# One encoder layer on one core: the buffers of the split weight blocks, each 64 bytes longer

## The chip, the cores and the metric

The kernel runs on one core of one Trainium2 chip. The metric is the device time of one execution in microseconds (us), the median of the runs shown. Lower is better.

## The reference

One layer of a hybrid encoder on 1024 tokens of width 1024, all in float32. Two gated feed-forward layers (`_swiglu`) stand around a mixing layer with bidirectional retention and a two-dimensional neighbourhood attention; each part has an RMS norm before and after it.

```python
def _swiglu(x, w_in, w_out):
    g, u = jnp.split(x @ w_in, 2, axis=-1)
    return (jax.nn.silu(g) * u) @ w_out
...
    h = _swiglu(_rms_norm(x, ffn1_pre_norm[l]), ffn1_w_in[l], ffn1_w_out[l])
    x = x + 0.5 * _rms_norm(h, ffn1_post_norm[l])
    m = _token_mixing(_rms_norm(x, mix_pre_norm[l]), w_mix_in[l], ret_decay_fwd[l], ret_decay_bwd[l],
                      na_rel_bias[l], w_ret_out[l], w_na_out[l], w_mix_out[l], pos)
    x = x + _rms_norm(m, mix_post_norm[l])
    h = _swiglu(_rms_norm(x, ffn2_pre_norm[l]), ffn2_w_in[l], ffn2_w_out[l])
    x = x + 0.5 * _rms_norm(h, ffn2_post_norm[l])
```

The weights are w_in 1024 x 5632, w_out 2816 x 1024, w_mix_in 1024 x 6656 and three output projections.

## The kernel before, in words

Every large product is made in a split form. A float32 operand a is written as h + l: h is a rounded to the matmul's input type (float32r) and l is the rest. A product of two split operands is three matmuls, h h, h l and l h (`mm3`, lines 86 to 90), summed in one bank of PSUM. A matmul has a stationary operand, 128 x 128, which a weight load (LDWEIGHTS, engine PEld in the profile) brings into the array first, and a moving operand of up to 512 columns, which streams through it. The weight load of a matmul runs while the matmul before it streams. In the profile's rows the moving operand stands first: `ps<-a11h,wh` has a11h moving and wh stationary.

Weight blocks come from HBM into `wraw` (`raw`, lines 70 to 73) and are split by `piece` (lines 75 to 80): ScalarE (ACT) writes the rounded block to a buffer `wh` and VectorE (DVE) the rest to a buffer `wl`, both 128 partitions x 512 columns. There are eight buffers of each, used in turn, and a piece takes one of each, so the two always have the same number. In the first feed-forward products and in the projections that use `Pairs` (a Winograd form: seven block products in place of eight), slices of 128 columns of `wh` and `wl` are stationary, and the split activations a11, a12, a22, s1 to s4 move; there a piece serves 4 slices x 3 matmuls = 12. In the second feed-forward products (`ffn_out`) the pieces move and the gated activations g are stationary, in 4 slices, again 12 matmuls for a piece. In the mixing layer's projections the pieces move or stand still as the place wants it, with 6 to 24 matmuls for a piece.

The order of the instructions is the order of the code, apart from a few high-priority regions; `Filler` interleaves projections with attention and retention.

Where the operands lie matters to the change. The tiles are given out from both ends of each partition's memory. Their lengths are whole multiples of 512 bytes per partition, but for small ones and for two paddings (`edge`, 128 bytes, and `pad` in `mix`, 160 bytes). In the built program all of wraw, wh, wl, t2, the a and s operands, g, xy, gh, gl, pth, vh, k, q and nearly every other large tile begin at an address that leaves 352 when divided by 512; the identity matrix of the transposes leaves 128, and `ev` in the mixing pool 0. This remainder is called the residue below.

One place reads within a tile at another residue: in the neighbourhood attention's scores (`scores` in `na_cores`, line 909) the moving operand is a window of k, 12 rows of 32 columns (128 bytes out of every 256), which begins 0, 32, 96 or 128 bytes behind the tile's start, by the column block (`KEY_OFF`); the stationary q stands at 352 there too. Line 65 has the subtraction of the split with a scale, `ql<-qraw,qh`: qraw is read in pieces of 64 bytes, 256 bytes apart, and qh and ql without a gap, so the two sources' residues differ by another amount from piece to piece.

Of the kernel before, what the change touches and what calls it, by code (L numbers as in the profile page):

```python
# [11 lines left out]
F32R = mybir.dt.float32r  # L12
# [6 lines left out]
P = 128  # L19
# [19 lines left out]
class Core:  # L39
# [34 lines left out]

    def piece(self, src, eng=None):

        h = self.wpool.tile([P, 512], F32R, tag="wh", name="wh", bufs=8)
        l = self.wpool.tile([P, 512], F32R, tag="wl", name="wl", bufs=8)
        self.split(h, l, src, eng=eng)
        return h, l  # L80

# [1502 lines left out]
```

## Time and profile before

| | |
|---|---|
| median of three timed runs | 2288.16 us (2287.96 to 2288.34) |
| span of the profiled execution, first to last instruction | 2285.9 us |
| what lies around the span (median less span) | 2.3 us |
| TensorE (PE) busy | 2210.8 us, 97% of the span, 10232 matmuls |
| weight loads (PEld) busy | 1828.4 us, 80% |
| VectorE (DVE), ScalarE (ACT), GpSimd (POOL) busy | 74%, 44%, 28% |
| mean granted TensorE clock | 0.991 of full speed |

The profile gives no time of its own for the profiled execution beside its span. A matmul's row gives the time from its start to its modelled end; matmuls overlap, so the time that one adds to a dense stretch is the distance between two starts, which is a window's length by the number of matmuls in it.

### The profile page before, as it was taken

To read this page: it belongs to the slowest core of one execution; us is meant where nothing else is said; L and a number is where in the kernel's file an instruction comes from. 1 tells how busy PE (TensorE), PEld (TensorE's weight loads), DVE (VectorE), ACT (ScalarE), POOL (GpSimd) and SP (SyncE) were. 2 spreads that over 40 slices of the span, in tenths; PEclk is the share of its full clock that TensorE was granted. 3 is DMA by queue.
4 is the path that set the end of the run, shared out by engine and by line. 5 is a ranking of instruction groups with operands and counts; after the bars stand their busy time and mean duration, and the time that the engine had idled before them with its cause. 6 is when DMAs were issued, how large, how long until landed. Compare 5 with 4: busy or idle time off the path is not lost. (4 is left out here: it accounts for less than half of the span.)

```text
span 2285.9 us, 30140 instructions
## 1 busy us (share of the span) xinstructions
PE 2210.8 (97%) x10232; PEld 1828.4 (80%) x10232; DVE 1686.3 (74%) x2928; ACT 1000.7 (44%) x2086; POOL 650.9 (28%) x779
## 2 busy tenths in 40 slices
PE   6899999999998999999999999999899999999998
PEld 5688888888787887778888888887578888888886
DVE  7998878755568667969876678537988888886444
ACT  5444434332344322259875665315544343433232
POOL 1121212169424133401101222101531212125942
PEclk9999999999999999999999999999999999999999
DMA  6353434597555452357754566766434444349865
GB/s 248 134 193 134 175 129 175 213 379 282 203 178 172 149 184 79 111 187 255 219 165 165 166 212 233 288 219 206 171 133 171 166 150 163 140 144 369 303 224 181
DMA packets 150090, 444.11 MB, mean 194 GB/s; under 512 B 18800, under 2 KB 46576, under 8 KB 147824
## 3 DMA queue, kind: packets, MB, share of 16 engines
q1 hardware_dynamic: 111216, 314.23, 40.2%
q0 software_dynamic: 38720, 127.96, 14.6%
q8 instruction: 81, 1.33, 0.2%
q14 instruction: 73, 0.60, 0.1%
HBM read 305.80 MB, written 140.51 MB: 195 GB/s over the span
## 5 line engine op out<-in xcount | busy, mean ns | idle before, releaser
L62 DVE TENSOR_TENSOR wl<-wraw,wh 128x512 fp32r<-128x512 f32 x512 | 363.9, 730 | 83.1 <-ACT wh L61 82.3
L61 ACT CAST wh<-wraw 128x512 fp32r<-128x512 f32 x516 | 297.9, 618 | 213.5 <-DVE wraw L530 63.8
L88 PE MATMUL ps<-wh,g 128*128 128x512 f32 x484 | 188.7, 390 | 0.0
L89 PE MATMUL ps<-wl,g 128*128 128x512 f32 x484 | 188.5, 389 | 0.0
L90 PE MATMUL ps<-wh,g 128*128 128x512 f32 x484 | 188.3, 389 | 0.0
L552 ACT ACTIVATE c<-c 128x512 f32<-128x512 f32 x88 | 55.5, 632 | 205.8 <-DVE c L517 105.8
L62 DVE TENSOR_TENSOR wl<-w,wh 128x512 fp32r<-128x512 f32 x77 | 75.5, 993 | 84.9 <-ACT wh L61 83.9
L62 DVE TENSOR_TENSOR wl<-x,wh 128x512 fp32r<-128x512 f32 x77 | 80.5, 1066 | 75.8 <-ACT wh L61 74.8
L61 ACT CAST wh<-t 128x512 fp32r<-128x512 f32 x58 | 36.0, 621 | 191.1 <-DVE t L511 191.0
L88 PE MATMUL ps<-a11h,wh 128*128 128x512 f32 x276 | 111.7, 405 | 7.5 <-ACT wh L61 7.3
L90 PE MATMUL ps<-a11h,wl 128*128 128x512 f32 x276 | 109.7, 398 | 5.0 <-DVE wl L62 4.9
L88 PE MATMUL ps<-a22h,wh 128*128 128x512 f32 x280 | 109.9, 392 | 0.0
L90 PE MATMUL ps<-a22h,wl 128*128 128x512 f32 x280 | 109.2, 390 | 0.6 <-DVE wl L62 0.6
L89 PE MATMUL ps<-a11l,wh 128*128 128x512 f32 x276 | 109.5, 397 | 0.1
L88 PE MATMUL ps<-a12h,wh 128*128 128x512 f32 x276 | 108.9, 394 | 0.3 <-ACT wh L61 0.3
L90 PE MATMUL ps<-a12h,wl 128*128 128x512 f32 x276 | 107.9, 391 | 1.3 <-DVE wl L62 1.3
L89 PE MATMUL ps<-a22l,wh 128*128 128x512 f32 x280 | 109.1, 390 | 0.0
L89 PE MATMUL ps<-a12l,wh 128*128 128x512 f32 x276 | 107.7, 390 | 0.0
L89 PEld LDWEIGHTS ps<-wl,g 128*128 128x128 f32 x484 | 90.9, 188 | 18.9 <-DVE wl L62 0.5
L90 PEld LDWEIGHTS ps<-wh,g 128*128 128x128 f32 x484 | 90.8, 188 | 18.9
L88 PEld LDWEIGHTS ps<-wh,g 128*128 128x128 f32 x484 | 90.8, 188 | 18.9
L68 POOL DMA_DIRECT2D g0a<-gth x33 | 18.0, 550 | 290.9 <-ACT gth L599 273.8
(435 smaller groups left out, 6540.1 us busy)
## 6 DMA issues: line engine op xcount, KB each, us to landing
wraw<-in_dram SPq DMA_DIRECT2D x218, 512.0 KB, 4.4
g<-g0s SPq DMA_DIRECT2D x44, 512.0 KB, 4.2
g<-g1s SPq DMA_DIRECT2D x44, 512.0 KB, 4.6
g<-g0a SPq DMA_DIRECT2D x33, 512.0 KB, 3.2
g<-g1a SPq DMA_DIRECT2D x33, 512.0 KB, 4.4
g0s<-gth POOLq DMA_DIRECT2D x44, 256.0 KB, 4.4
g0s<-cmb POOLq DMA_DIRECT2D x44, 256.0 KB, 3.7
g1s<-gth POOLq DMA_DIRECT2D x44, 256.0 KB, 4.5
```

The lines of the kernel that those rows point to most:

```text
L61: self.done = [nc.scalar.copy(h, src).ins, (eng or nc.vector).tensor_tensor(l, src, hf, ALU.subtract).ins]
L62: (eng or nc.vector).tensor_tensor(l, src, hf, ALU.subtract).ins]
L68: self.nc.gpsimd.dma_start(dst, src)
L88: mm(ps, a[0], b[0], start=start, stop=False)
L89: mm(ps, a[0], b[1], start=False, stop=False)
L90: mm(ps, a[1], b[0], start=False, stop=stop)
L552: nc.scalar.activation(gate[j], gate[j], AF.Silu)
```

## The change

The buffers of `wh` and `wl` are made 528 columns long (2112 bytes per partition in place of 2048), and the first 512 columns of each are used. No instruction, order, size of an operation or number of buffers is changed; the five engines' orders are the same, row by row, in both programs. In the built program the buffers of `wh`, in turn, now leave the residues 352, 416, 480, 32, 96, 160, 224 and 288, and those of `wl` the same in the same order, as eight buffers of 2112 bytes are a whole multiple of 512. All tiles behind them lie 1024 bytes higher and keep their residue.

```diff
     def piece(self, src, eng=None):
 
-        h = self.wpool.tile([P, 512], F32R, tag="wh", name="wh", bufs=8)
-        l = self.wpool.tile([P, 512], F32R, tag="wl", name="wl", bufs=8)
+        h = self.wpool.tile([P, 528], F32R, tag="wh", name="wh", bufs=8)[:, :512]
+        l = self.wpool.tile([P, 528], F32R, tag="wl", name="wl", bufs=8)[:, :512]
         self.split(h, l, src, eng=eng)
         return h, l
```

## The prediction

> **What bounds the kernel now.** I read the page first, then stretches of the run in the table by stage, then the groups of matmuls within those stretches. The page's engine row and the stages:
>
> ```profile
> PE 2210.8 (97%) x10232; PEld 1828.4 (80%) x10232; DVE 1686.3 (74%) x2928; ACT 1000.7 (44%) x2086; POOL 650.9 (28%) x779
> ```
>
> The columns of the stages are: window, its length, then for PE, PEld, DVE, ACT and POOL the busy time and the number of instructions, the clock and the DMA.
>
> ```profile
> 1000.00:1160.00 160.00, 154.49 (x870) 133.22 (x869) 141.26 (x408) 128.86 (x332) 18.95 (x27) 1.00 0.73 232
> 1440.00:1555.00 115.00, 115.00 (x509) 95.24 (x508) 53.27 (x82) 27.23 (x46) 6.15 (x11) 1.00 0.71 253
> 1720.00:2060.00 340.00, 340.00 (x1502) 281.53 (x1501) 282.51 (x457) 136.54 (x242) 67.74 (x126) 1.00 0.44 158
> ```
>
> TensorE is the bound. From 1720 to 2060 us (first half of the second feed-forward layer) it has no idle time at all: 1502 matmuls, two of them cut by the window's edges, so 340.00 / 1500 = 226.7 ns from start to start. From 1440 to 1555 us, where the retention's output projection and the next one follow each other, it is 115.00 / 508 = 226.4 ns, the same within the edges. DVE is busy 282.51 of 340 us there and ACT 136.54, so both have room. A change in a matmul's pace therefore goes to the end of the kernel one to one; a change on DVE or ACT does not, as long as it stays within that room.
>
> The pace is not the same everywhere. Groups of matmuls within the windows; the number behind the bar is busy time in us, then the mean of one in ns:
>
> ```profile
> L89 PE MATMUL ps<-xy,wh 128*128 128x512 f32 x128 | 49.8, 389 | 0.0
> ```
>
> ```profile
> L88 PE MATMUL ps<-wh,a21h 128*128 128x512 f32 x30 | 11.8, 394 | 0.0
> L89 PE MATMUL ps<-wl,a21h 128*128 128x512 f32 x30 | 11.8, 394 | 0.0
> L90 PE MATMUL ps<-wh,a21l 128*128 128x512 f32 x30 | 11.7, 392 | 0.0
> ```
>
> The first is from 1440 to 1555 us, the other three from 1000 to 1160 us, where short groups of them stand between the attention's smaller matmuls. All have 512 columns, no idle time ahead of them and the full clock, yet these take 392 to 394 ns against 389. So a matmul of 512 columns has a steady pace and a slightly slower one, and what stood before it on the same engine has a say in which it gets. That is the size of effect this change can have on a row that otherwise never waits.
>
> **The change part by part.** It removes and adds no instruction, wait or transfer. It moves where 16 buffers begin, and three engines touch these.
>
> VectorE and ScalarE. The split writes wh on ACT and then reads wraw and wh together on DVE; both sources stood at one residue, now they do for one buffer in eight. Rows of line 62 (minimum, median and maximum in ns):
>
> ```profile
> L62 DVE TENSOR_TENSOR wl<-wraw,wh x512: 674/685/1808, 30.5 to 2050.0; 128x512 fp32r<-128x512 f32 x171
> L62 DVE TENSOR_TENSOR wl<-x,wh x77: 676/693/5617, 456.2 to 662.1; 128x512 fp32r<-128x512 f32 x77
> L62 DVE TENSOR_TENSOR wl<-w,wh x77: 676/693/1832, 2066.5 to 2255.7; 128x512 fp32r<-128x512 f32 x77
> L62 DVE TENSOR_TENSOR vl<-vraw,vh x76: 415/420/695, 1032.3 to 1421.8; 128x256 fp32r<-128x256 f32 x60, 128x512 fp32r<-128x512 f32 x16
> L62 DVE TENSOR_TENSOR wl<-t,wh x58: 677/692/695, 54.9 to 2042.7; 128x512 fp32r<-128x512 f32 x58
> ```
>
> The trace has one DVE operation whose two sources lie at differing residues, line 65's:
>
> ```profile
> L65 DVE SCALAR_TENSOR_TENSOR ql<-qraw,qh x32: 417/420/1521, 1023.3 to 1170.3; 128x256 fp32r<-128x256 f32 x32
> ```
>
> It has 256 columns and takes 420 ns, as `vl<-vraw,vh` does with 256 columns and one residue. I cost the subtraction at nothing. If it did grow, the cover is DVE's free 57 us in the 340 above: 107 or so splits fall there, so each could grow by half a microsecond before TensorE would wait. ACT's cast reads one source and writes one target; its room is larger. Nothing is taken for either.
>
> TensorE. Each piece feeds 12 matmuls, as stationary or as moving operand, and in all of these the other operand stays at 352. Pieces: 512 + 77 + 77 + 58 = 724 by the rows above (three more are split on GpSimd), and 724 x 12 = 8688 matmuls of 512 columns, nearly all of the 10232 but the short ones. One buffer in eight keeps its residue, so 7602 matmuls get operands at different residues. No matmul of 512 columns in the trace of before is like that, so the price has to be bounded. The nearest rows are the scores of the attention, 384 columns, where the moving window of k begins 0, 32, 96 or 128 bytes off the residue of the stationary q. Offset 0 (two units, 1062 to 1069 us):
>
> ```profile
> L909 PE MATMUL ps<-k,qh x4: 338/338/339, 1062.6 to 1068.4; 128*128 128x384 f32 x4
> L909 PE MATMUL ps<-k,ql x4: 339/341/343, 1062.8 to 1068.6; 128*128 128x384 f32 x4
> ```
>
> Offset 128 (two units, 1094 to 1100 us):
>
> ```profile
> L909 PE MATMUL ps<-k,qh x4: 338/340/343, 1094.1 to 1099.7; 128*128 128x384 f32 x4
> L909 PE MATMUL ps<-k,ql x4: 343/344/344, 1094.3 to 1099.8; 128*128 128x384 f32 x4
> ```
>
> Offset 96 (1078 to 1079 us), where the medians are 340 and 342:
>
> ```profile
> L909 PE MATMUL ps<-k,qh x2: 339/340/342, 1078.4 to 1078.8; 128*128 128x384 f32 x2
> L909 PE MATMUL ps<-k,ql x2: 342/342/342, 1078.6 to 1079.0; 128*128 128x384 f32 x2
> ```
>
> The medians' means are 339.5 ns at offset 0, 341 at 96 and 342 at 128. The shape, the stationary operand and the work ahead are the same; what differs is the offset. The offset of 128 is the only one that is a multiple of 64 bytes, as all of the change's are, so I take its 2.5 ns for 384 columns, and 2.5 x 512 / 384 = 3.3 ns for 512. Sum: 7602 x 3.3 = 25 us. It is close to what the stage from 1000 to 1160 us shows between the two paces, 394 - 389 = 5 ns and 392 - 389 = 3 ns, and lies on the path all the way. The ends: below, 387 ns is the shortest of its kind against the usual 389, 2 ns less; above, the longest of a group that never waits is 397, 8 ns more:
>
> ```profile
> L88 PE MATMUL ps<-a22h,wh x280: 387/389/504, 72.2 to 2063.6; 128*128 128x512 f32 x140
> L88 PE MATMUL pt<-wh,g x132: 389/389/397, 488.2 to 2246.0; 128*128 128x512 f32 x132
> ```
>
> So the ends are -15 us and +61 us, and nothing between them is excluded by a row.
>
> The weight load itself has room: 188 ns by the row below, under a matmul of 226.7 ns, and the next one can only start with the next matmul. A slower load costs nothing until it grows by some 39 ns.
>
> ```profile
> L88 PEld LDWEIGHTS ps<-wh,g x484: 187/188/190, 456.5 to 2275.7; 128*128 128x128 f32 x162
> ```
>
> The waits of TensorE for splits stay as they are, since neither the splits nor their order change. Part of a slower pace would vanish in them, but they are few: TensorE's idle time is 2285.9 - 2210.8 = 75 us, 3% of the span, so under 1 us of the 25. The sum is made on the profiled span, 2285.9 + 25 = 2310.9 us, and with the 2.3 us by which the median of the runs is above that span, 2313 us.
>
> **The rivals.** First, no change: the two streams of TensorE do not meet at all, and the 2.5 ns of the scores come from the window's pieces of 128 bytes. For it speaks that the scores at offset 32 are within 0.5 ns of offset 0 (340 and 340 against 338 and 341), and that all large groups have the same 389 ns whether the pieces move or stand still:
>
> ```profile
> L909 PE MATMUL ps<-k,qh x2: 340/340/340, 1073.2 to 1073.6; 128*128 128x384 f32 x2
> L909 PE MATMUL ps<-k,ql x2: 339/340/341, 1073.4 to 1073.8; 128*128 128x384 f32 x2
> ```
>
> Against it speaks that offset 0 and offset 128 cut the window into the same kinds of pieces and still differ. Time: 2288 us. The Trainium skill, "TensorE: Matmul & The Clock Gate", section "Step-by-step: what each phase is for", sides with this rival: TensorE is said to have two independent read ports into SBUF, one for the moving operand and one for weight loads, and a load is said to take no bandwidth from the running matmul. By that rule the sum would be nothing; the rows at offsets 0 and 128 do not fit it well, but no row decides it.
>
> Second, faster: the steady pace of 226.7 ns is itself what two streams at one residue cost each other, and streams at different residues meet less. The shortest row, 387 ns, is 2 ns below the usual; 7602 x 2 = 15 us less, 2273 us. The point from which it decides is simple: it wins if the matmuls of the seven shifted buffers start less than 226.7 ns apart. Against it: at one residue 389 is met with hardly any spread, and the offsets of the scores go the other way. The same page of the Trainium skill, section "Back-to-back issue gap", gives N / 2.4 + 2.5 ns for a matmul of N columns, 215.8 ns for 512; the trace's 226.7 does not agree, and if the difference of 10.9 ns were due to the shared residue, the gain would be up to 83 us, 2205 us. No row shows such a pace for 512 columns.
>
> Third, slower by more than forecast: after every change of buffer the streams fall out of pace and stay there for all 12 matmuls, at 397 in place of 389 ns. 7602 x 8 = 61 us, 2349 us. For it: 397 occurs in a group without waits. Against it: the stage from 1000 to 1160 us, broken up every few matmuls, means only 394.
>
> That the change does not do what it says is no rival: the addresses of the built program are as the change has them.
>
> **How the numbers follow.** A measurement of this kernel can tell about 0.2%, 4.6 us, from no change. Forecast (+25 us, slower): 0.45. Slower by more: 0.18. No change: 0.22. Faster: 0.15. So slower by over 0.2% has 0.63, within 0.2% 0.22, faster 0.15. The likeliest is 2313 us. The range must leave out no more than 0.2: it takes in no change and the forecast whole, goes up to the third rival's 2349 us, which leaves out about half of its 0.18, and down to 2280 us, half of the way to the second rival's 2273 and beyond no change, which leaves out about 0.11. For the slower cases alone it would be 2293 to 2349.
>
> **What would show it.** Right: in the stage from 1720 to 2060 us, 1480 matmuls in 340 us in place of 1502 (230 ns each), `ps<-xy,wh` at about 392 in place of 389 ns, the idle times and the DVE row at 685 ns unchanged, and within a stage runs of 12 matmuls of differing pace. The first rival: all rows as they are. The second: more than 1502 matmuls in the window. The third: 397 ns throughout. The forecast is wrong if the matmuls keep 226.7 ns, or if DVE's subtraction leaves 685 ns by more than half a microsecond and TensorE begins to wait for it.

## The result and the profile after

The changed kernel takes 2315.57 us (median of 4 runs, 2314.12 to 2318.32), the kernel before 2288.06 us (2287.73 to 2288.34) on the same chip. The ratio is 1.0115, interval 1.0099 to 1.0132: slower by 27.5 us, six times the 4.6 us below which the prediction counts a difference as no change. The profiled execution's span went from 2285.9 to 2313.0 us, 27.1 us more.

The page's engine row of the changed kernel, busy time and number of instructions:

```profile
PE 2243.2 (97%) x10232; PEld 1831.3 (79%) x10232; DVE 1687.1 (73%) x2928; ACT 1001.3 (43%) x2086; POOL 649.9 (28%) x779
```

TensorE's busy time grew by 32.4 us (from 2210.8) with the same 10232 instructions. DVE, ACT and POOL stayed within 1 us, and the weight loads (PEld) within 3 us. The changed kernel's stage from 1720 to 2060 us (window, its length, then PE, PEld, DVE, ACT, POOL, clock, DMA):

```profile
1720.00:2060.00 340.00, 338.78 (x1470) 275.81 (x1469) 283.27 (x459) 135.98 (x241) 68.20 (x128) 1.00 0.44 156
```

It holds 1470 matmuls, where there were 1502. It is still almost without idle time and at the full clock. (The work stands up to 27 us later by now, but the window lies within one stage in both kernels.) The group that the prediction watched, minimum, median and maximum in ns:

```profile
L89 PE MATMUL ps<-xy,wh x128: 388/392/404, 1457.0 to 1544.6; 128*128 128x512 f32 x128
```

The same group before:

```profile
L89 PE MATMUL ps<-xy,wh x128: 389/389/389, 1440.6 to 1526.7; 128*128 128x512 f32 x128
```

All 128 of these took 389 ns. Now the median is 392 and single ones spread from 388 to 404. The splits of line 62 in the changed kernel:

```profile
L62 DVE TENSOR_TENSOR wl<-wraw,wh x512: 672/684/1814, 30.1 to 2073.1; 128x512 fp32r<-128x512 f32 x171
L62 DVE TENSOR_TENSOR wl<-x,wh x77: 676/734/1785, 462.3 to 671.9; 128x512 fp32r<-128x512 f32 x77
```

The large group has 684 ns, where it had 685. The small one, `wl<-x,wh`, went from a median of 693 to 734, which is not where the time went: c64 below has 695 in that row and loses more.

For a finer measure I took, in each trace, the distance from the start of every 512-column matmul to the start of the next, leaving out those above 245 ns (a wait or a change of shape; some 250 in each kernel). These 8550 to 8600 pairs have a mean of 227.29 ns before and 231.06 ns after. Over 8583 pairs that is 1950.8 us before and 1983.2 after, 32.4 us more. The rest of the time between the first and the last matmul's start gave 4.8 us back (314.2 to 309.4 us, waits above all), hence the 27.

### The profile page after: what moved, and what is told of

It is laid out like the page before. It is cut to its first block, busy times and chain, and to the rows that moved or that the text cites. A ratio compares the mean times of both kernels' runs of the same rounds, so it can differ in the third digit from the quotient of the medians.

```text
span 2313.0 us, 30140 instructions
## 1 busy us (share of the span) xinstructions
PE 2243.2 (97%) x10232; PEld 1831.3 (79%) x10232; DVE 1687.1 (73%) x2928; ACT 1001.3 (43%) x2086; POOL 649.9 (28%) x779
## 4 chain that ended last, share of the span: by engine, by line
PE 79%; DVE 10%; issue 5%; ACT 3%; POOL 2%; DMA 2%; POOLq 0%; SPq 0%; DVEq 0%; ACTq 0%
PE ps L90 24%; PE ps L88 24%; PE ps L89 24%; DVE wl L62 2%; PE pt L88 1%; PE pt L89 1%; PE pt L90 1%; POOL rstd L98 1%; PE ps L909 1%; PE pt L928 1%; ACT wh L61 1%; DVE t L511 1%; DMA wraw<-in_dram 0%; DVE tmp L118 0%; DMA g0a<-gt 0%
```

## The experiments

Theory: a matmul's pace depends on the distance, in bytes and modulo some period, between the residues of its stationary and its moving operand. The rivals: (A) only a step from one buffer to another with a different residue costs; (B) the loss comes from DVE and the splits; (C) any distance but 0 costs the same; (D) the residue itself counts, of whichever operand. All the kernels here run the kernel before's instructions, in its order on each of the five engines (in c128 alone two VectorE instructions of one small tile, lines 990 and 997, change places); what differs is addresses. Their times stand against the kernel before on their own chip (2291 us, in the last two runs 2289 us).

**One distance for all buffers.** A gap of N columns ahead of `wh`, and 128 - N behind `wl`, moves all 16 buffers alike and leaves everything else at its residue (352 for the operands). For 64, 128 and 256 bytes N is 16, 32 and 64:

```diff
-
-        h = self.wpool.tile([P, 512], F32R, tag="wh", name="wh", bufs=8)
-        l = self.wpool.tile([P, 512], F32R, tag="wl", name="wl", bufs=8)
+        gap = lambda n, w: setattr(self, n, getattr(self, n, None) or [self.wpool.tile([P, w], F32, name=n)])
+        gap("gap1", 16); h = self.wpool.tile([P, 512], F32R, tag="wh", name="wh", bufs=8)
+        l = self.wpool.tile([P, 512], F32R, tag="wl", name="wl", bufs=8); gap("gap2", 112)
```

c64: 

> All buffers of wh and wl begin 64 bytes off the residue of the other operands (416 against 352), buffer after buffer the same. Theory (the pace of a matmul goes by the distance of its moving from its stationary operand, modulo 256 bytes): in the trace of the changed kernel the matmuls at a distance of 64 start 229 to 230 ns apart against 226.7, so 8688 x 2.5 to 3 ns = 22 to 26 us more, about 2312 us. Rival A (it is the step from one buffer's residue to the next that costs, streams then fall back into step): no steps here, 2288 us. Rival B (DVE's subtraction suffers from wraw and wh at different residues): its row leaves 685 ns.

c128: 

> The same with 128 bytes (480 against 352). Theory: matmuls at a distance of 128 start 232 to 233 ns apart in the trace of the changed kernel, so 8688 x 5.5 ns = 48 us more, about 2336 us, more than the changed kernel itself. Rival A (only steps cost): 2288 us. Rival C (any distance costs the same): as much as the run with 64 bytes.

c256: 

> The same with 256 bytes (96 against 352). Theory with a period of 256 bytes: 2288 us, no change. Rival with a period of 512 bytes, as the change's own words suggest: a loss at least as at 128 bytes, 2336 us or more.

Measured: c64 2322.57 us, ratio 1.0145 (1.0123 to 1.0166); c128 2328.04 us, 1.0165 (1.0147 to 1.0183); c256 2292.37 us, 1.0005 (0.9991 to 1.0019). A shift by 256 bytes costs nothing, so the period is 256 bytes and not the 512 of the change's wording. Neither c64 nor c128 has any step between buffers, and both lose more than the changed kernel: rival A, as the only cause, falls. c64 lies above what its theory expected (2312), c128 below (2336). The rows of c64, two with W (the split weight pieces) stationary (`xy,wh` and `xy,wl`) and then one with W moving (`wh,g`):

```profile
L89 PE MATMUL ps<-xy,wh x128: 393/398/398, 1462.2 to 1550.9; 128*128 128x512 f32 x128
L90 PE MATMUL ps<-xy,wl x128: 392/393/398, 1462.5 to 1551.1; 128*128 128x512 f32 x128
L88 PE MATMUL pt<-wh,g x132: 388/392/394, 499.3 to 2284.4; 128*128 128x512 f32 x132
```

The first of these rows in c256:

```profile
L89 PE MATMUL ps<-xy,wh x128: 389/389/389, 1445.9 to 1532.0; 128*128 128x512 f32 x128
```

And the splits in c64:

```profile
L62 DVE TENSOR_TENSOR wl<-wraw,wh x512: 672/684/1807, 31.2 to 2086.2; 128x512 fp32r<-128x512 f32 x171
L62 DVE TENSOR_TENSOR wl<-x,wh x77: 676/695/1825, 467.1 to 674.7; 128x512 fp32r<-128x512 f32 x77
```

DVE's rows are those of before (685 and 693) in a kernel that loses 1.45%: rival B falls. (In all32 below, which loses nothing, the small row has a median of 714; it moves without the loss, too.) In c64 the matmuls with W stationary are the slower ones. Counted from the stationary operand to the moving one, modulo 256, their distance is 352 - 416 = -64, so 192, and that of the others 64. This suggested that the sign counts.

**All operands moved.** The gap of 32 columns now stands ahead of everything, and the tile `edge` is 128 columns wide, so that W and all other operands begin at 480:

```diff
-    c.small = const
-    pad = edge.tile([P, 32], F32, name="edge")
+    c.small = const; wpool.tile([P, 32], F32, name="gap1")
+    pad = edge.tile([P, 128], F32, name="edge")
```

> Every large tile, wh and wl with the others, begins 128 bytes higher (residue 480 in place of 352), so the distances are 0 as before. Theory (the distance counts): 2288 us. Rival D (the residue itself counts, and 352 is a good one for wh and wl): as the run that shifts wh and wl alone by 128, about 2336 us.

Measured: 2289.8 us, ratio 1.0000 (0.9989 to 1.0010). The residue by itself costs nothing; rival D falls for 128 bytes. all32 does the same with 8 and 24 columns, which puts every operand at 384, a multiple of 64 bytes:

> All operands of the matmuls, W and the others alike, begin 32 bytes further on, so that all distances stay at 0 while every operand now begins on a multiple of 64. If only the distance between operands counts: no change, 2290. If the start within 64 bytes counts by itself: another time, faster if the 512 columns then cover a step fewer, by up to the 3.3 ns of one step for each of 8.6 thousand matmuls (2262).

Measured: 2290.08 us, ratio 0.9997 (0.9985 to 1.0008), and in all32's stage from 1720 to 2060 us:

```profile
1720.00:2060.00 340.00, 340.00 (x1502) 281.52 (x1501) 285.06 (x461) 135.85 (x241) 67.80 (x127) 1.00 0.45 156
```

The 1502 matmuls of before, to the unit. Its expectation left room for a time below that of the kernel before, and that did not come.

**The sign, and finer distances.** c192, c32 and c96 have N = 48, 8 and 24 in the first diff (and 128 - N behind). c192 swaps the distances of c64: 64 with W stationary, 192 with W moving.

c192: 

> Both halves of W (wh, wl) begin 192 bytes further on, all 16 buffers alike; every other operand stays where it is. If the matmul's pace follows the signed distance modulo 256 from the stationary operand to the moving one: matmuls with W stationary (distance 64) go as in c64's other half, 229.5 ns, those with W moving (distance 192) 233 ns. From 227.3 that is 5840 x 2.2 + 2740 x 5.9 = 29 us: about 2318 against 2290, and less than the loss of c64 (31.5), with the kinds of matmul changed about. If only the size of the distance counts, whichever way: the kinds stay as in c64 (W stationary slow, W moving less so).

c32: 

> wh and wl begin 32 bytes further on. If the pace is a matter of steps of 64 bytes: W stationary and W moving are each either at distance 0 or at one step, so the time lies between no change (2290) and c64's (2322). If the pace changes evenly with the distance, half of c64's loss: about 2306. If a distance as such costs nothing and the overlap of reads can also be better than at 0: below 2290.

c96: 

> wh and wl begin 96 bytes further on, so that matmuls with W stationary stand at distance 160 (modulo 256, from the stationary operand to the moving one) and those with W moving at 96. The distances tried so far cost, against 227.3 ns at 0: 2 ns at 64, 5.3 at 128, 6 at 192, and 6 at 32 and 224. If odd multiples of 32 cost alike: 6 ns for all, like c32 (2330). If the cost follows from the neighbouring multiples of 64: 5.3 to 6 ns with W stationary, 2 to 5.3 with W moving, about 2325. A time below 2290 would show a better distance than 0.

Measured: c192 2310.52 us, ratio 1.0090 (1.0073 to 1.0107); c32 2330.01 us, 1.0173 (1.0156 to 1.0190); c96 2336.99 us, 1.0213 (1.0196 to 1.0230). The same three rows in c192:

```profile
L89 PE MATMUL ps<-xy,wh x128: 390/394/394, 1455.7 to 1542.7; 128*128 128x512 f32 x128
L90 PE MATMUL ps<-xy,wl x128: 388/388/392, 1455.9 to 1542.9; 128*128 128x512 f32 x128
L88 PE MATMUL pt<-wh,g x132: 393/394/398, 493.8 to 2272.2; 128*128 128x512 f32 x132
```

With W moving the median went from 392 in c64 to 394; with W stationary it went from 398 to 394 on line 89 and from 393 to 388 on line 90. The rows alone overlap; the start-to-start times in the table below do not: W stationary goes from 233.3 ns in c64 to 229.2 in c192, and W moving from 229.4 to 233.4. The sign counts, and c192 is the cheapest of the shifts that cost anything, since two thirds of the matmuls have W stationary. That rules out rival C. c32's rows:

```profile
L89 PE MATMUL ps<-xy,wh x128: 395/395/396, 1462.9 to 1551.5; 128*128 128x512 f32 x128
L88 PE MATMUL pt<-wh,g x132: 393/394/397, 500.2 to 2286.7; 128*128 128x512 f32 x132
```

The expectation had no case above c64's time, and c32 lies above it: 32 bytes are worse than 64. c96, too, lies above both of its cases (2330 and 2325). From the start-to-start times (mean over 2700 to 5900 matmuls in each place):

| distance, stationary to moving, modulo 256 | start to start, ns | from |
|---|---|---|
| 0 | 227.3 | before, c256, all128, all32 |
| 32 | 233.3 | c32, W moving |
| 64 | 229.2, 229.4 | c192, W stationary; c64, W moving |
| 96 | 233.3 | c96, W moving |
| 128 | 232.5, 232.9 | c128, W stationary; W moving |
| 160 | 234.1 | c96, W stationary |
| 192 | 233.3, 233.4 | c64, W stationary; c192, W moving |
| 224 | 233.3 | c32, W stationary |

Three distances (64, 128 and 192) were met with W in both roles, and there the two agree within 0.4 ns, so it is the distance and not the role. Of the eight distances 0 is the best, and the kernel before has it in all its matmuls of 512 columns: none of the other distances in steps of 32 bytes beats it.

**Whose distance, and the cost of a step.** wl64 moves `wl` alone by 64 bytes, with the gap between the two sets of buffers (`gap` is defined as in the first diff; that line is left out here):

```diff
         h = self.wpool.tile([P, 512], F32R, tag="wh", name="wh", bufs=8)
-        l = self.wpool.tile([P, 512], F32R, tag="wl", name="wl", bufs=8)
+        gap("gap1", 16); l = self.wpool.tile([P, 512], F32R, tag="wl", name="wl", bufs=8); gap("gap2", 112)
```

> Only wl begins 64 bytes further on; wh and all else stay. A piece has three matmuls per operand block: two use wh, one uses wl. If the distance between a matmul's own two operands sets its pace: only the matmuls with wl slow down (to about 233 ns with wl stationary, 229.5 with wl moving), a third of c64's loss of 31.5 us: about 2301. If it is the weights that load beside it that count (the next matmul's stationary operand): the matmul just ahead of the one with wl slows down, by as much, and the one with wl keeps 227. If any two operands that differ within a piece cost (a change of residue from one matmul to the next): all three slow down, and the loss is near c64's.

Measured: 2317.0 us, ratio 1.0115 (1.0100 to 1.0130), where a third of c64's loss would be 2301. The three matmuls of a triple in wl64:

```profile
L88 PE MATMUL ps<-xy,wh x128: 389/389/397, 1457.7 to 1545.8; 128*128 128x512 f32 x128
L89 PE MATMUL ps<-xy,wh x128: 388/392/394, 1458.2 to 1546.0; 128*128 128x512 f32 x128
L90 PE MATMUL ps<-xy,wl x128: 389/397/398, 1458.4 to 1546.2; 128*128 128x512 f32 x128
```

Line 90 has the shifted `wl` as its own stationary operand and goes from 389 to 397 ns. Line 89, beside which `wl` is loaded, gains 3 ns, and line 88 nothing in the median. In start-to-start times, over all matmuls with W stationary, it is 228.8, 229.5 and 235.1 ns for lines 88, 89 and 90, against 227 each before. So the expectation that the matmul with `wl` itself slows down holds for its place, but its price is 8 ns and not 6, and its neighbours pay some 2 ns each though their own operands are at distance 0. With W moving all three pay (231.5, 232.1 and 232.4 ns), though only the second has a shifted operand. A change of distance from one matmul to the next thus has a price as well, and in wl64, where it comes twice in every three matmuls, it is the larger part: the kernel loses 26 us where the distances alone would have given 10. A caution stays: ends of matmuls in the trace are modelled, and a slow interval cannot be told from one that began a matmul earlier and shows late. So whether a moving operand's distance counts to its own stationary operand, or to the one that is loaded beside it, is not settled: in the kernels with one distance for all buffers the two are the same, and wl64 points to its own only if the intervals are taken as they stand.

len544 makes the buffers 128 bytes longer in place of 64, otherwise as the change does:

```diff
-        h = self.wpool.tile([P, 512], F32R, tag="wh", name="wh", bufs=8)
-        l = self.wpool.tile([P, 512], F32R, tag="wl", name="wl", bufs=8)
+        h = self.wpool.tile([P, 544], F32R, tag="wh", name="wh", bufs=8)[:, :512]
+        l = self.wpool.tile([P, 544], F32R, tag="wl", name="wl", bufs=8)[:, :512]
```

> The buffers of wh and wl are 128 bytes longer instead of 64, so that they begin at four residues modulo 512, which are two distances modulo 256: 0 and 128. With the period of 256 and each matmul priced by its own distance: half of the matmuls at 0, half at 5.3 ns, 2.65 x 8575 = 23 us, about 2313. If each step from buffer to buffer costs too (0.5 ns per matmul by what remains of the change's own 3.8 ns after its four distances): 27 us, about 2317. If the period were 512 or larger: the four residues 0, 128, 256 and 384, three quarters of the matmuls slow, 34 us, about 2325.

Measured: 2313.1 us, ratio 1.0107 (1.0090 to 1.0124). The four residues are two kinds: 4253 matmuls at distance 0 have a mean of 228.3 ns, 4313 at distance 128 have 232.7. So the period is 256 here too. Split further, matmuls whose neighbours have the same distance take 227.9 and 232.4 ns, those next to a step 231.1 and 234.4. The 1146 at a step thus cost 3.2 and 1.9 ns more, 530 x 3.2 + 616 x 1.9 = 2.9 us of the kernel's 24. The price reaches past the neighbours: at distance 0 the first three matmuls behind a step have a mean of 230.8 ns, and from the eighth on it is 227.1, so that distance 0 as a whole lies 1.0 ns above the 227.3 of before, 4.3 us. The steps are real, and small where they are as rare as here, 518 among 8832 matmuls.

The theory stands, with a period of 256 bytes and a sign, and with a term for steps, the part of rival A that survives: small where a piece serves many matmuls at one distance, the larger part in wl64, where the distance changes within every triple.

## Why the prediction was right, step by step

The bound was right: TensorE almost without idle time, 1502 matmuls in the 340 us before and 1470 after, and 27 of the 32 us of slower pace went to the end. So was the VectorE step: the large row kept its 685 ns to within 1 ns, the 77 splits `wl<-x,wh` grew by 41 ns in the median, far less than the half microsecond that the prediction left them, and c64 shows DVE's rows unmoved in a slower kernel.

The TensorE step was right in its mechanism: the two operands' residues set the pace. It counted 7602 matmuls at one price of 3.3 ns, 25 us. Its two factors were both off, in opposite directions, and the price is not one but goes by the distance. With the period of 256, two of the eight buffers (352 and 96) stand at distance 0, not one: 6439 of the 8583 matmuls are shifted, by the changed kernel's addresses laid beside its trace. Their prices against 227.29 ns:

| own distance in the changed kernel | matmuls | start to start, ns | more, us |
|---|---|---|---|
| 0 | 2144 | 228.5 | 2.7 |
| 64 | 2107 | 230.2 | 6.2 |
| 128 | 2126 | 232.4 | 10.9 |
| 192 | 2206 | 233.0 | 12.6 |

The sum is 32.4 us. A distance of 128 costs 5 ns where the scores' rows gave 3.3 (2.5 for 384 columns, scaled up). The unshifted quarter pays 1.2 ns, as it stands between shifted pieces: the first three matmuls behind a step take 230.5 ns there, those from the eighth on 227.2. The steady prices of the distance table would have given (0 + 2.0 + 5.4 + 6.0) / 4 = 3.4 ns per matmul. The 3.8 measured leave 0.4 ns, some 4 us, for the steps; they lie in the rows of 0 and 64, while those of 128 and 192 are no dearer than in the distance table.

The term for TensorE's waits was too small: under 1 us was to vanish in them, and 4.8 us did in the profiled execution. With it 32.4 becomes 27.6, near the forecast's 25. That the total met the measurement within 3 us is in part the luck of these errors.

The views that were to show it: 1480 matmuls were expected from 1720 to 2060 us and 1470 stand there; `ps<-xy,wh` was expected at about 392 ns and has that median; DVE's large row was to stay at 685 and has 684; differing paces from piece to piece are there (table above).

The rivals. No change fell, and with it the reading of the scores on which it leaned: their offset of 32 was within 0.5 ns of offset 0, yet in the dense stages 32 bytes cost 6 ns (c32). Rows of the scores have the sign and the order of size of the effect at 128 bytes, but not its shape: at offset 96, too, they gave 1.5 ns in the mean where c96 gives 6. The Trainium skill, "TensorE: Matmul & The Clock Gate", section "Step-by-step: what each phase is for", sided with this rival by its two independent read ports; the runs do not agree, since moving one operand by 32 to 224 bytes costs 2 to 7 ns a matmul while moving both costs none. Faster fell: no distance in steps of 32 bytes gave a quicker pace than one residue does. Slower with 397 ns throughout fell for this kernel, though a steady shift of 96 bytes does reach that median: in c96 line 89's `ps<-xy,wh` has 392, 397 and 400 ns as minimum, median and maximum.

## What to carry to other kernels

In a stretch where matmuls stand back to back with a weight load beside each, place the stationary and the moving operands at the same residue modulo 256 bytes; which residue it is made no difference here (352, 384 and 480 modulo 512 were tried for all operands). The runs show this for 128 x 128 and 128 x 512 operands in float32r. Padding a buffer by less than 256 bytes can cost 1 to 2% of such a kernel without adding an instruction, and it shows in the rows and start-to-start times of the matmuls alone, not in idle time. A price taken from a short, broken-up group tells that an effect exists; its size and shape in the dense stage have to be measured in the dense stage.

## What was not expected

The period is 256 bytes (227.3 ns at 256 as at 0), and the effect has a sign: the moving operand 64 bytes ahead of the stationary one costs 2 ns, 64 bytes behind it 6. Distances of 32 bytes either way cost 6 ns, more than 64 ahead. What in the reading of the two operands makes this pattern is not settled by these runs; the weight load itself does not get longer. It took 188 ns before; in c32's page its row (busy time, mean, PEld's idle time ahead) reads:

```profile
L88 PEld LDWEIGHTS ps<-wh,g 128*128 128x128 f32 x484 | 90.7, 187 | 22.1
```

The load keeps to 187 ns while the matmuls around it are 6 ns slower, so the loss does not come from a longer load that a matmul then waits for.
